# Inverting the triangular blocks of an RWKV recurrence in two stages: side 16 on VectorE, side 32 on TensorE

## The chip, the cores and the metric

The kernel runs on one core of a Trainium2 chip. The metric is the device time of one execution in microseconds (us). A core has TensorE (PE in the profile, with its weight loads as PEld), VectorE (DVE), ScalarE (ACT), GpSimd (POOL) and SyncE (SP), which here only issues transfers.

## What is computed

The program is a two-layer backbone (model width 1024, 256 latent and 256 context tokens, 4-byte floats). Layer 0 has retention beside grouped-query attention and a dense feed-forward part; layer 1 has differential attention beside a bidirectional RWKV-7 recurrence, and then top-2-of-8 experts. The change touches the recurrence. For each of 8 heads of width 64 and in each of two directions, the reference runs over the tokens:

```python
def step(s, inp):
    rt, wt, kt, vt, at, bt = inp
    s_new = (s * wt[:, :, None, :]
             + jnp.einsum('bhvk,bhk->bhv', s, at)[..., None] * bt[:, :, None, :]
             + vt[..., None] * kt[:, :, None, :])
    y = jnp.einsum('bhvk,bhk->bhv', s if read_before else s_new, rt)
    return s_new, y
```

The kernel computes this in chunks of 64 tokens. Inside a chunk, the term with `a` and `b` makes each token depend on the earlier ones of the chunk, which is a unit triangular system of side 64 for each chunk, head and direction. The kernel inverts these matrices ahead of the scan.

## The kernel before

Tokens come in two halves of 256, half 0 the context and half 1 the latent tokens. A half has 4 chunks, 8 heads and 2 directions: 64 triangular matrices of side 64, each with two diagonal blocks of side 32 and one block off the diagonal. The stages of `layer1` from about 840 to 1090 us of the profile, in their order:

- `prep(d, half)` makes the decayed operands AR (`a` and `r`) and BK (`b` and `k`) of a direction, with ScalarE's exponentials and sigmoids and, on VectorE, scalings of 256 elements (L966) and operations of 1024 (L950, L962 to L972).
- `inv_blocks(half)` (L992) makes the diagonal blocks (`dg`, L1008) and those off the diagonal (`off`, L1011) by small products on quadrants of the array, copies them to Lc and Lo on ScalarE, and with a transpose of 32x32 blocks on VectorE (L1018) brings Lc into M: one diagonal block of side 32 to a partition, 128 in all.
- `inv_diag(half, cut)` (L1022) inverts all 128 blocks at once by forward substitution, N = (I - M)^-1, in 31 steps. A step is a product (tile tmv or tmg, L1037) and an addition into N (L1039). The columns of N below `cut` are VectorE's, the others GpSimd's; `cut` is 2 for half 0 and 8 for half 1.
- `inv_join(half)` (L1044) turns N back with two transposes on VectorE (X0 and X1, L1048 and L1049), copies the blocks into XF (L1055), and finds the block off the diagonal with two sets of 64 small products, `gp` (L1063) and `wp` (L1072). ScalarE copies gp to Gs and wp into XF (L1077).
- `chain(half)` runs the recurrence, four times a step for both directions. `step` (L1111) has products lm, transposes tp, then z (from the state), u (XF times z), s (the new state), and for half 1 the output Y.

`weave` writes several generators side by side: the inversion of half 0 beside prep and inv_blocks of half 1, the inversion and joining of half 1 beside chain(0). chain(1) follows, then the output projection with `moe_open`, which starts the stream of expert weights (L1411) that runs to the end. The order in which an engine gets its instructions is set by a scheduler of the framework from this program; each engine then works in that order. PSUM banks are named by use (`banks`): before, `acc` takes three banks in turn during the inversion of half 0 and then six.

Of the kernel before, what the change touches and what calls it, by code (L numbers as in the profile page):

```python
# [19 lines left out]
FFN = 2816  # L20
# [8 lines left out]
# columns of a diagonal block's inversion that the vector engine takes from GpSimd, per half  # L29
CUT0, CUT1 = 2, 8  # L30
# how the modulation is spread: over the FFN (yields, start), with gqa, with the retention
# [3 lines left out]
# buffers that hold weights until their own use comes, and the last chunk that may lie there  # L35
# [3 lines left out]
def _constants():  # L39
# [18 lines left out]
    parts["hind"] = hind.reshape(128, 32)  # L58
    def rope(dim):
        rows = SEQ // GRID_W  # L60
        row = np.repeat(np.arange(rows, dtype=f), GRID_W)
        col = np.tile(np.arange(GRID_W, dtype=f), rows)
        n = dim // 4
        fr = f(10000.0) ** (-np.arange(n, dtype=f) / f(n))
        ang = np.concatenate([row[:, None] * fr, col[:, None] * fr], axis=-1).astype(f)
        return np.cos(ang).astype(f), np.sin(ang).astype(f)
# [29 lines left out]
def weave(*parts):  # L96
    """emits generators side by side; each part is (generator, its number of yields, where it starts)"""
    live = [[float(at[0]) if at else 0.0, i, g, n] for i, (g, n, *at) in enumerate(parts)]
    while live:
        p = min(live)  # L100
        try:
            next(p[2])
            p[0] += 1.0 / p[3]
        except StopIteration:
            live.remove(p)
# [25 lines left out]
def _build(top, tc, nc, V, S, G, T, I, O):  # L131
# [22 lines left out]
    def banks(**by_use):  # L154
        """which PSUM banks each use takes in turn"""
        use.update(by_use)
# [7 lines left out]
    acc, tpp, att, ybank = (bank(k) for k in ("acc", "tp", "at", "y"))  # L164
    banks(acc=range(6), tp=(6, 7))
# [32 lines left out]
    def columns(name, parts):  # L198
        """the given rows of 128 as columns"""
        n = sum(p[2] for p in parts)  # L200
        rows = xnp0.tile([n, 128], F32, name=name + "_r")
        r0 = 0
        for nm, src, k in parts:
            nc.scalar.dma_start(rows[r0:r0 + k], src)
            voff[nm] = r0
            r0 += k
        out = const_([128, n], name)
        t0 = tpp()
        T.transpose(t0[:, 0:n], rows, ident[0:n, 0:n])
        V.tensor_copy(out, t0[:, 0:n])  # L210
        return out
# [65 lines left out]
    def mod(layer):  # L277
# [4 lines left out]
        def put(q, tv):  # L282
            """section q in columns, as the norms' scales and shifts"""
            if q == 1:
                o = voff["ng"] + layer * 32
                ng = vec[:, o:o + 8].rearrange("p (s b) -> p b s", s=2)
                for r in range(2):
                    V.scalar_tensor_tensor(by_half(A1)[:, :, :, r], tv[:, :, :, r], 1.0, ng, op0=ALU.add, op1=ALU.mult)
            else:
                V.tensor_copy(by_half({0: B1, 3: B2, 4: A2}[q]), tv[:, :, :, 0:2])  # L290
# [12 lines left out]
        def first_two(pool):  # L303
            """sections 0 and 1 on the tensor engine: row r of slice s of 512 on partition 32 s + r"""
# [18 lines left out]
        def section(q):  # L323
            """1024 modulation columns, the products on the vector engine and their sums over the partitions on the
            tensor engine: row r of half s on partition 32 s + r, from section 2 on with the norm's factor:
            gate * g | shift | (1 + scale) * g | gate * g"""
# [41 lines left out]
        def rowb(pool, n, r, name, tag=None, q=nc.scalar):  # L368
            """section n's row for stream r on all partitions"""
            t = pool.tile([128, D], F32, name=name, tag=tag or name, bufs=1)  # L370
            bcast_rows(t, I["mrow"][layer, n // 2 - 1, r, n % 2 * 1024:n % 2 * 1024 + 1024], q)
            return t
# [3 lines left out]
    def norm_stats(xnp, blks):  # L376
        """rstd [128, blocks] and the normalized blocks"""
# [31 lines left out]
    def proj_tok(wsrc, n0, blks, fin, off=0, chunks=range(4), src=None, bmajor=False, out=None, spare=None):  # L409
        """token-major h @ w[:, n0:n0+512]; fin(b, PSUM tile) takes each block"""  # L410
# [24 lines left out]
    def post_norm_add(xnp, y, b, gb):  # L435
        """X[:, b] += rmsnorm(y) * gb with y two PSUM banks or SBUF halves"""
# [44 lines left out]
    def softmax(pool, sc, n, scale):  # L481
        """normalized exp over the free axis of a PSUM score tile"""
# [233 lines left out]
    def ffn0(first):  # L716
# [26 lines left out]
        def down(half, blks):  # L743
            """the blocks, both column halves, added to what the other half left"""
# [15 lines left out]
        def down_all(half):  # L760
            """all blocks, a column half at a time"""
# [29 lines left out]
    def layer1():  # L791
# [33 lines left out]
        def shift(i, a, dst, segs):  # L825
            """token shift of feature tile i from PSUM a[:, segs * 256] to dst [128, segs, 256]"""
# [8 lines left out]
        def project(i0):  # L835
            """feature-major tiles i0, i0 + 1 of the shifted projection"""
# [49 lines left out]
        def lora_weights(d):  # L886
            """rows of the other direction are zero, and so is what it adds"""
# [10 lines left out]
        def unit_keys():  # L898
            """minus the keys: k * k_k over its norm per head, which is found once per head and spread by a product"""
# [23 lines left out]
        def prep(d, half):  # L923
            """decayed operands of a direction: AR = (a | r), BK = (b | k), feature-major by chunk"""
# [63 lines left out]
        bn = lambda name: qI.tile([128, 32, 32], F32, name=name, tag="bn", bufs=5)  # L988
# [3 lines left out]
        def inv_blocks(half):  # L992
            """the 32 x 32 diagonal blocks of all chunks of a half, one to a partition, and those off the diagonal"""
            Lc = bn("Lc")
            off = acc("off")
# [21 lines left out]
            M = bn("M")  # L1017
            V.transpose(M.rearrange("p r c -> p c r"), Lc.rearrange("p u c -> p c u"))  # L1018
            iv[half] = M, Lo
            yield  # L1020

        def inv_diag(half, cut):  # L1022
            """forward substitution, columns shared by two engines: N becomes the inverse of I - M in each partition"""
            M, Lo = iv[half]
            N = bn("N")
            G.memset(flat(N), 0.0)
            G.memset(flat(N)[:, 0:1024:33], 1.0)
            for t in range(31):
                for eng, name, j0, j1 in ((V, "tmv", 0, cut), (G, "tmg", cut, 31)):
                    j1 = min(j1, t + 1)  # L1030
                    if j1 <= j0:
                        continue
                    tm = qI.tile([128, 256], F32, name=name, tag=name, bufs=2)
                    n, m = 31 - t, j1 - j0
                    tv = tm[:, 0:n * m].rearrange("p (i j) -> p i j", i=n)
                    Nv = N[:, t + 1:32, j0:j1]
                    eng.tensor_tensor(tv, M[:, t + 1:32, t:t + 1].to_broadcast([128, n, m]),  # L1037
                                      N[:, t:t + 1, j0:j1].to_broadcast([128, n, m]), op=ALU.mult)
                    eng.tensor_tensor(Nv, Nv, tv, op=ALU.add)  # L1039
                yield  # L1040
            iv[half] = N, Lo
            yield

        def inv_join(half):  # L1044
            """XF: transposed inverses of the unit triangular systems of all chunks of a half"""
            N, Lo = iv[half]
            X0, X1 = bn("X0"), bn("X1")
            V.transpose(X0.rearrange("p u c -> p c u"), N.rearrange("p r c -> p c r"))  # L1048
            V.transpose(X1.rearrange("p u r -> p r u"), N)  # L1049
            yield  # L1050
# [7 lines left out]
            Gs = qI.tile([128, 16, 32], F32, name="Gs", tag="Gs", bufs=1)  # L1058
# [22 lines left out]
        banks(acc=(3, 4, 5), at=(0, 1, 2))  # L1081
        drain(inv_blocks(0))
        weave((seq(prep(0, 1), prep(1, 1), inv_blocks(1)), 19), (inv_diag(0, CUT0), 32))
# [4 lines left out]
        for b in range(2):  # L1088
# [3 lines left out]
            V.tensor_copy(bon[:, b], t[:, 0:8])  # L1092
        banks(acc=range(6))
        drain(inv_join(0))
# [117 lines left out]
        weave((chain(0), 16), (seq(inv_diag(1, CUT1), inv_join(1)), 32))  # L1212
# [20 lines left out]
        def finish():  # L1233
            """what the last steps need besides the scan: (y * ln_g + ln_b + bonus) * gate = y * G1 + G2"""
# [68 lines left out]
    def diff(W, oD):  # L1303
        """projects for the differential attention; its pool and a generator of the attention"""
# [76 lines left out]
    def moe_open(rowb):  # L1381
        """what the experts need early: the stream of their weights and the modulation rows"""
# [30 lines left out]
        def ahead(c):  # L1413
            """loads what has its place free once chunk c - 1 is used"""
# [19 lines left out]
    def route_weights():  # L1434
        """logits = rstd * (x @ rt) + rb"""
# [8 lines left out]
    def moe():  # L1444
# [21 lines left out]
        def pre_split(eng=V):  # L1466
            """the next chunk into hi and lo parts, one [128, n] pair per row block"""
# [13 lines left out]
        def marks(g, q):  # L1481
            """one-hot: which row goes to which place of experts 2 g and 2 g + 1"""
# [22 lines left out]
        def warm(n):  # L1505
            """keeps the array's clock up where it would wait"""
# [11 lines left out]
        def turned(b):  # L1518
            """a block feature-major, and its sums of squares"""
# [92 lines left out]
        def gate_weights():  # L1612
            """softmax of the two logits, and the counts"""
# [19 lines left out]
        def gather(g, k2s=range(4)):  # L1633
            """the rows of experts 2 g and 2 g + 1, side by side, feature-major"""
# [136 lines left out]
    def sqrt_table():  # L1771
        """has the table of the last norm loaded ahead of it"""
# [3 lines left out]
    def overflow(mc, h2, gts, slotv, cnt, cmx, yacc, wg, wu, wd):  # L1776
        """rows of an expert beyond its first 128"""
# [96 lines left out]
```

## Time and profile before

| | us |
|---|---|
| three runs | 2152.70, 2155.31, 2157.81 |
| median | 2155.31 |
| profiled execution, first to last instruction | 2153.4 |
| TensorE busy | 2045.5 (95%) |
| VectorE busy | 1663.8 (77%) |
| ScalarE busy | 1220.2 (57%) |
| GpSimd busy | 166.0 (8%) |

The profile is one execution; its span is 1.9 us below the median of the runs. "Busy" is the time in which an instruction of that engine ran. A share over the whole span mixes stages with different limits, so stretches and timelines are read below. In a timeline, a row can stand for several equal instructions (x64); a bracket gives the idle time of the engine ahead of it and what ended that. "issue" means that nothing that the profile shows ended it. The granted clock (PEclk) is TensorE's, 1.00 for 2.4 GHz and 0.50 for 1.2 GHz.

### The profile page before, as it was taken

To read this page: it belongs to the slowest core of one execution; us is meant where nothing else is said; L and a number is where in the kernel's file an instruction comes from. 1 tells how busy PE (TensorE), PEld (TensorE's weight loads), DVE (VectorE), ACT (ScalarE), POOL (GpSimd) and SP (SyncE) were. 2 spreads that over 40 slices of the span, in tenths; PEclk is the share of its full clock that TensorE was granted. 3 is DMA by queue.
4 is the path that set the end of the run, shared out by engine and by line. 5 is a ranking of instruction groups with operands and counts; after the bars stand their busy time and mean duration, and the time that the engine had idled before them with its cause. 6 is when DMAs were issued, how large, how long until landed. Compare 5 with 4: busy or idle time off the path is not lost. (4 is left out here: it accounts for less than half of the span.)

```text
span 2153.4 us, 30029 instructions
## 1 busy us (share of the span) xinstructions
PE 2045.5 (95%) x11521; PEld 1635.4 (76%) x11522; DVE 1663.8 (77%) x2099; ACT 1220.2 (57%) x1581; POOL 166.0 (8%) x223
## 2 busy tenths in 40 slices
PE   6999989999999999858999999999999999999997
PEld 2767778777887766748887888888888787888875
DVE  3977783674557556688568999889989999899987
ACT  3543342222235445633337777777777777777775
POOL 0211110000000110284001000000000000000000
PEclk8999999999999999969999999999999999999999
DMA  8435351475645331101077999999999999999993
GB/s 297 160 109 168 110 172 55 152 244 187 203 150 166 111 88 45 36 16 51 21 268 258 366 317 350 332 347 367 355 343 352 350 372 347 339 352 357 366 353 144
DMA packets 224202, 493.99 MB, mean 229 GB/s; under 512 B 11355, under 2 KB 45262, under 8 KB 224054
## 3 DMA queue, kind: packets, MB, share of 16 engines
q1 hardware_dynamic: 219968, 482.62, 64.4%
q10 hardware_dynamic: 4086, 9.40, 1.3%
q8 instruction: 92, 1.51, 0.3%
q14 instruction: 56, 0.46, 0.1%
HBM read 490.87 MB, written 1.11 MB: 228 GB/s over the span
## 5 line engine op out<-in xcount | busy, mean ns | idle before, releaser
L273 DVE TENSOR_TENSOR mlo<-mraw,mhi 128x1024 fp32r<-128x1024 f32 x668 | 789.1, 1221 | 79.2 <-ACT mhi L272 62.4
L272 ACT ACTIVATE mhi<-mraw 128x1024 fp32r<-128x1024 f32 x668 | 682.9, 1057 | 104.3 <-PE y L269 49.0
L262 ACT ACTIVATE whi<-raw 128x1024 fp32r<-128x1024 f32 (+1 forms) x150 | 153.0, 1024 | 279.6 <-PE acc L269 109.6
L263 DVE TENSOR_TENSOR wlo<-raw,whi 128x1024 fp32r<-128x1024 f32 (+1 forms) x146 | 175.1, 1203 | 137.8 <-ACT whi L262 137.4
L267 PE MATMUL acc<-hTh,whi 128*128 128x512 f32 (+1 forms) x504 | 190.7, 380 | 0.0
L268 PE MATMUL acc<-hTl,whi 128*128 128x512 f32 (+1 forms) x504 | 186.6, 371 | 0.0
L269 PE MATMUL acc<-hTh,wlo 128*128 128x512 f32 (+1 forms) x504 | 185.6, 369 | 0.0
L268 PE MATMUL g<-mlo,xh 128*128 128x512 f32 x448 | 182.5, 407 | 0.3 <-POOL mlo L1581 0.3
L337 DVE SCALAR_TENSOR_TENSOR part<-mraw,cond,part 128x1024 f32<-128x1024 f32 x112 | 147.8, 1341 | 40.3 <-DMA mraw<-in_mod_w 40.2
L267 PE MATMUL g<-mhi,xh 128*128 128x512 f32 x448 | 178.6, 399 | 0.0
L267 PE MATMUL u<-mhi,xh 128*128 128x512 f32 x448 | 177.3, 396 | 0.0
L268 PE MATMUL u<-mlo,xh 128*128 128x512 f32 x448 | 177.3, 396 | 0.0
L269 PE MATMUL u<-mhi,xl 128*128 128x512 f32 x448 | 177.1, 395 | 0.0
L269 PE MATMUL g<-mhi,xl 128*128 128x512 f32 x448 | 177.1, 395 | 0.0
L268 PE MATMUL y<-mlo,acts 128*128 128x512 f32 x448 | 175.7, 392 | 0.3 <-DVE mlo L273 0.3
L269 PE MATMUL y<-mhi,acts 128*128 128x512 f32 x448 | 174.8, 390 | 0.0
L267 PE MATMUL y<-mhi,acts 128*128 128x512 f32 x448 | 151.4, 390 | 0.0
L267 PE MATMUL acc<-whi,hTh 128*128 128x512 f32 x336 | 137.7, 413 | 5.3 <-ACT whi L262 3.4
L268 PE MATMUL acc<-wlo,hTh 128*128 128x512 f32 x336 | 135.8, 404 | 4.5 <-DVE wlo L263 4.5
L269 PE MATMUL acc<-whi,hTl 128*128 128x512 f32 x336 | 134.7, 402 | 0.0
L267 PEld LDWEIGHTS acc<-hTh,whi 128*128 128x128 f32 x504 | 95.3, 190 | 22.4 <-issue 4.1
L268 PEld LDWEIGHTS acc<-hTl,whi 128*128 128x128 f32 x504 | 95.0, 189 | 17.6 <-issue 2.8
(437 smaller groups left out, 3510.1 us busy)
## 6 DMA issues: line engine op xcount, KB each, us to landing
mraw<-in_moe_w_gate SPq DMA_DIRECT2D x112, 1024.0 KB
mraw<-in_moe_w_up SPq DMA_DIRECT2D x112, 1024.0 KB
mraw<-in_moe_w_down SPq DMA_DIRECT2D x110, 1024.0 KB
mraw<-in_mod_w SPq DMA_DIRECT2D x96, 512.0 KB
raw<-in_ffn_w_down SPq DMA_DIRECT2D x32, 512.0 KB
raw<-in_odd_w_in SPq DMA_DIRECT2D x26, 512.0 KB
raw<-in_even_w_in SPq DMA_DIRECT2D x24, 512.0 KB
raw<-in_ffn_w_gate SPq DMA_DIRECT2D x20, 512.0 KB
```

The lines of the kernel that those rows point to most:

```text
L262: S.activation(h, v, AF.Copy)
L263: (eng or V).tensor_tensor(l, v, h, op=ALU.subtract)
L267: T.matmul(out, ah, bh, start=first, stop=False)
L268: T.matmul(out, ah, bl, start=False, stop=False)
L269: T.matmul(out, al, bh, start=False, stop=last)
L272: S.activation(hi, src, AF.Copy)
L273: eng.tensor_tensor(lo, src, hi, op=ALU.subtract)
L337: V.scalar_tensor_tensor(part[r], w, c_, part[r], op0=ALU.mult, op1=ALU.add)
```

## The change

Each diagonal block of side 32 is taken as two blocks of side 16 on the diagonal and one off it. `inv_diag` inverts the two blocks of 16 in each partition with the same VectorE operations (a further axis x of 2), in 15 steps; GpSimd has no part in it. The block off the diagonal is then found by TensorE in `inv_join`: `dc` is Lc times the right half of X1, ScalarE copies it to DC (with a mask of 0 and 1 by row, a new constant low16), and two sets of products, both called x, give what is added into X0 and X1. Each set has 128 products with a stationary 32x32 and a moving 32x16, on the four diagonal quadrants of the array in turn. After that the joining to side 64 goes on as before. The big tiles now have named places (`places`) in place of a ring of five, `acc` has two banks and then five where it had three and six, and `off` has a bank of its own.

```diff
-        bn = lambda name: qI.tile([128, 32, 32], F32, name=name, tag="bn", bufs=5)
+        places = ({"M": 0, "N": 1, "X0": 3, "X1": 0, "DC": 1, "Gs": 1}, {"M": 2, "N": 3, "X0": 0, "X1": 1, "DC": 2, "Gs": 2})
+        bnt = lambda name, half: qI.tile([128, 2, 528], F32, name=name, tag=f"bn{places[half][name]}", bufs=1)
+        whole = lambda x: x.rearrange("p x f -> p (x f)")[:, 0:1024].rearrange("p (a b) -> p a b", a=32)
+        diag16 = lambda x: x[:, :, 0:512].rearrange("p x (r c) -> p x r c", c=32)[:, :, :, 0:16]
+        bn = lambda name, half: whole(bnt(name, half))
...
-            for t in range(31):
-                for eng, name, j0, j1 in ((V, "tmv", 0, cut), (G, "tmg", cut, 31)):
-                    j1 = min(j1, t + 1)
-                    if j1 <= j0:
-                        continue
-                    tm = qI.tile([128, 256], F32, name=name, tag=name, bufs=2)
-                    n, m = 31 - t, j1 - j0
-                    tv = tm[:, 0:n * m].rearrange("p (i j) -> p i j", i=n)
-                    Nv = N[:, t + 1:32, j0:j1]
-                    eng.tensor_tensor(tv, M[:, t + 1:32, t:t + 1].to_broadcast([128, n, m]),
-                                      N[:, t:t + 1, j0:j1].to_broadcast([128, n, m]), op=ALU.mult)
-                    eng.tensor_tensor(Nv, Nv, tv, op=ALU.add)
+            Md, Nd = diag16(M), diag16(N)
+            for t in range(15):
+                tm = qI.tile([128, 128], F32, name="tmv", tag="tmv", bufs=2)
+                n, m = 15 - t, t + 1
+                tv = tm[:, 0:2 * n * m].rearrange("p (x i j) -> p x i j", x=2, i=n)
+                Nv = Nd[:, :, t + 1:16, 0:m]
+                V.tensor_tensor(tv, Md[:, :, t + 1:16, t:t + 1].to_broadcast([128, 2, n, m]),
+                                Nd[:, :, t:t + 1, 0:m].to_broadcast([128, 2, n, m]), op=ALU.mult)
+                V.tensor_tensor(Nv, Nv, tv, op=ALU.add)
                 yield
...
             V.transpose(X1.rearrange("p u r -> p r u"), N)
             yield
+            quads = [(32 * x, u) for u in range(32) for x in range(4)]
+
+            def small(name, lhs, rhs):
+                a = acc(name)
+                for o_, u in quads:
+                    T.matmul(a[o_:o_ + 32, u * 16:u * 16 + 16], lhs[o_:o_ + 32, u], rhs[o_:o_ + 32, u],
+                             start=True, stop=True, tile_position=(o_, o_))
+                return a.rearrange("p (u r) -> p u r", u=32)
+            DC = bn("DC", half)
+            G.memset(DC[:, :, 0:16], 0.0)
+            a = small("dc", Lc, X1[:, :, 16:32])
+            S.activation(DC[:, :, 16:32], a, AF.Copy, scale=rc("low16"))
+            yield
+            a0 = small("x0", DC, X0[:, :, 0:16])
+            a1 = small("x1", X0, DC[:, :, 16:32])
+            V.tensor_tensor(X0[:, :, 0:16], X0[:, :, 0:16], a0, op=ALU.add)
+            V.tensor_tensor(X1[:, :, 16:32], X1[:, :, 16:32], a1, op=ALU.add)
+            yield
...
-        banks(acc=(3, 4, 5), at=(0, 1, 2))
+        banks(acc=(3, 4), at=(0, 1, 2), off=(5,))
         drain(inv_blocks(0))
-        weave((seq(prep(0, 1), prep(1, 1), inv_blocks(1)), 19), (inv_diag(0, CUT0), 32))
+        weave((seq(prep(0, 1), prep(1, 1), inv_blocks(1)), 19), (inv_diag(0), 16))
...
+        banks(acc=range(5))
+        drain(inv_join(0))
         banks(acc=range(6))
-        drain(inv_join(0))
...
-        weave((chain(0), 16), (seq(inv_diag(1, CUT1), inv_join(1)), 32))
+        weave((chain(0), 16), (seq(inv_diag(1), inv_join(1)), 21))
```

How the scheduler's order moves is seen at two places of TensorE's queue (an operation is named by the tile that it writes, then those that it reads; x counts products; the line numbers are those of the kernel before or of the changed one, which stand some 23 lines apart).

TensorE at the joining of half 0, before:

```order
L1139 MATMUL tp<-cst_all,vT 128x128 x4
L1126 MATMUL lm<-pad_7760,BK_6335 128x128 x4
L1132 MATMUL tp<-cst_all,BK_6338 128x128 x4
L1139 MATMUL tp<-cst_all,vT 128x128 x4
L1132 MATMUL tp<-cst_all,BK_6335 128x128 x4
L1149 MATMUL z<-UV,Lm 64x64 x8
L1139 MATMUL tp<-cst_all,vT 128x128 x2
L1063 MATMUL gp<-X_7608,Lo 32x32 x32
L1139 MATMUL tp<-cst_all,vT 128x128 x2
L1132 MATMUL tp<-cst_all,BK_6338 128x128 x2
```

The same place with the change:

```order
L1162 MATMUL tp<-cst_all,vT 128x128 x4
L1155 MATMUL tp<-cst_all,BK_6338 128x128
L1060 MATMUL dc<-X_7474,Lc 32x16 x128
L1155 MATMUL tp<-cst_all,BK_6338 128x128 x3
L1162 MATMUL tp<-cst_all,vT 128x128 x4
L1060 MATMUL x_7609<-X_7473,DC 32x16 x128
L1060 MATMUL x_7738<-DC,X_7473 32x16 x128
L1155 MATMUL tp<-cst_all,BK_6335 128x128 x4
L1162 MATMUL tp<-cst_all,vT 128x128 x4
L1085 MATMUL gp<-X_7473,Lo 32x32 x32
L1085 MATMUL gp<-X_7474,Lo 32x32 x32
```

The products lm and z of the recurrence stood between and ahead of gp. Now dc and both x come ahead of gp, the transposes tp between them, and lm and z behind.

TensorE at the end of the recurrence over half 0, before:

```order
L1152 MATMUL z<-St,pad_7763 64x64
L1162 MATMUL u<-zpad_7764,XF_6860 64x64 x8
L1139 MATMUL tp<-cst_all,vT 128x128 x2
L1063 MATMUL gp<-X_8447,Lo 32x32 x12
L1172 MATMUL s<-UV,bkt 64x64
L1162 MATMUL u<-zpad_7765,XF_6860 64x64
L1172 MATMUL s<-UV,bkt 64x64
L1063 MATMUL gp<-X_8447,Lo 32x32 x3
L1162 MATMUL u<-zpad_7765,XF_6860 64x64 x7
L1063 MATMUL gp<-X_8447,Lo 32x32 x16
L1172 MATMUL s<-UV,bkt 64x64 x8
```

The same place with the change (17 more of dc stand ahead of the z):

```order
L1172 MATMUL z<-UV,Lm 64x64
L1175 MATMUL z<-St,pad_8020 64x64
L1060 MATMUL dc<-X_8542,Lc 32x16 x111
L1185 MATMUL u<-zpad_8021,XF_6860 64x64 x8
L1185 MATMUL u<-zpad_8022,XF_6860 64x64 x8
L1060 MATMUL x_8699<-X_8541,DC 32x16 x128
L1060 MATMUL x_8828<-DC,X_8541 32x16 x128
L1195 MATMUL s<-UV,bkt 64x64 x16
L1085 MATMUL gp<-X_8541,Lo 32x32 x32
L1085 MATMUL gp<-X_8542,Lo 32x32 x32
```

gp was mixed with the last u and s. Now dc stands ahead of u, both x between u and s, and all of gp behind s.

## Rows read from the trace of the kernel before

**Rows 1.** The page: busy time of the engines; an instruction queue (packets, MB, share).

```profile
PE 2045.5 (95%) x11521; PEld 1635.4 (76%) x11522; DVE 1663.8 (77%) x2099; ACT 1220.2 (57%) x1581; POOL 166.0 (8%) x223
...
q8 instruction: 92, 1.51, 0.3%
```

**Rows 2.** Busy us (x instructions) of PE, PEld, DVE, ACT, POOL; PEclk, DMA share, GB/s.

```profile
930.00:950.00 20.00, 8.44 (x215) 8.30 (x216) 19.34 (x40) 0.60 (x1) 18.26 (x23) 0.50 0.07 15
...
970.00:1010.00 40.00, 36.37 (x565) 34.25 (x561) 33.69 (x98) 13.48 (x30) 14.37 (x35) 0.96 0.05 16
```

**Rows 3.** Timeline of VectorE (start us, us, line, operation), with one row on tile tmv.

```profile
905.05 2.07 DVE L1018 STREAM_TRANSPOSE M<-Lc 128x1024 f32<-128x1024 f32 x1 [4.46 <-ACT Lc L1013]
...
913.83 1.21 DVE L962 TENSOR_TENSOR BK<-tb,En 128x1024 f32<-128x1024 f32 x1
914.96 0.50 DVE L1037 TENSOR_TENSOR tmv<-M,N 128x50 f32<-128x50 f32 x1
...
945.48 0.47 DVE L1086 SCALAR_TENSOR_TENSOR rkT<-rT,vec,kT 128x256 f32<-128x256 f32 x1
...
961.55 0.15 DVE L1039 TENSOR_TENSOR N<-N,tmv 128x2 f32<-128x2 f32 x1
...
963.67 1.99 DVE L1049 STREAM_TRANSPOSE X<-N 128x1024 f32<-128x1024 f32 x1
...
L1037 DVE TENSOR_TENSOR tmv<-M,N x62: 144/298/632, 907.2 to 1007.1; 128x31 f32<-128x31 f32 x2, 128x60 f32<-128x60 f32 x2, 128x56 f32<-128x56 f32 x2, 128x48 f32<-128x48 f32 x2
```

**Rows 4.** Timelines of TensorE and ScalarE, joining of half 0, first z.

```profile
964.29 1.20 PE L1063 MATMUL gp<-X,Lo 32*32 32x32 f32 x64
...
966.00 1.20 PE L1063 MATMUL gp<-X,Lo 32*32 32x32 f32 x64
...
975.80 0.76 PE L1149 MATMUL z<-UV,Lm 128*64 128x64 f32 x13 [3.05 <-DVE Lm L1128]
...
971.00 2.40 ACT L1077 ACTIVATE XF<-wp 32x512 f32<-32x512 f32 x4 [0.40 <-PE wp L1072]
```

**Rows 5.** TensorE, dg and off: timeline, and two stretches (columns as in rows 2).

```profile
895.26 0.76 PE L1008 MATMUL dg<-BK,AR 64*32 64x32 f32 x64
...
897.98 0.25 PE L1008 MATMUL dg<-BK,AR 64*32 64x32 f32 x5 [0.75 <-issue]
...
901.98 0.28 PE L1008 MATMUL dg<-AR,BK 64*32 64x32 f32 x5 [2.45 <-issue]
...
897.90:901.90 4.00, 1.55 (x128) 1.44 (x128) 2.68 (x4) 1.60 (x4) 0.00 (x0) 0.98 0.24 64
...
937.00:940.70 3.70, 3.61 (x192) 3.53 (x192) 3.70 (x7) 0.00 (x0) 3.54 (x3) 0.50 0.02 4
```

**Rows 6.** DMA in 894 to 908 us: rate in 40 slots, and the instruction queue.

```profile
GB/s 0 0 0 0 0 47 0 0 0 0 0 0 0 0 0 0 47 0 70 211 181 140 123 23 0 0 0 47 0 0 0 0 0 0 0 0 0 0 47 0
...
q8 instruction: 4, 0.07, 1.6%
```

**Rows 7.** Timelines of TensorE and ScalarE, joining of half 1, first product of chain(1).

```profile
1017.38 1.89 PE L1072 MATMUL wp<-X,Gs 32*32 32x32 f32 x77 [0.47 <-issue]
1022.51 0.77 PE L1126 MATMUL lm<-pad,BK 128*128 128x256 f32 x1 [3.24 <-DVE pad L1118]
...
1019.31 2.38 ACT L1077 ACTIVATE XF<-wp 32x512 f32<-32x512 f32 x4 [2.38 <-PE wp L1072]
```

**Rows 8.** What starts the expert weights: SyncE's waits and issues, and three stretches.

```profile
SPq L240 <- PE Y L1189: 19.3, 1, 19.3
...
1090.99 1.38 SPq L1411 DMA_DIRECT2D mraw<-in_moe_w_gate  x1
...
1040.00:1060.00 20.00, 20.00 (x278) 18.20 (x277) 11.02 (x22) 6.52 (x14) 1.48 (x2) 1.00 0.01 2
1100.00:1110.00 10.00, 9.24 (x51) 7.51 (x50) 7.11 (x9) 3.20 (x4) 0.00 (x0) 1.00 1.02 374
2000.00:2100.00 100.00, 100.00 (x443) 80.33 (x442) 89.49 (x87) 75.78 (x83) 0.00 (x0) 1.00 0.99 357
```

More of the change, by code (lines that the diff above doesn't have):

```diff
@@ L28 @@
 RAW = 8
-CUT0, CUT1 = 2, 8
 NM, N0 = 72, 0.1
@@ L58, in _constants @@
     parts["hind"] = hind.reshape(128, 32)
+    parts["low16"] = (i[:, None] % 32 < 16).astype(f)
     def rope(dim):
@@ L164, in _build @@
     acc, tpp, att, ybank = (bank(k) for k in ("acc", "tp", "at", "y"))
+    offb = bank("off")
     banks(acc=range(6), tp=(6, 7))
@@ L992, in inv_blocks @@
         def inv_blocks(half):
-            Lc = bn("Lc")
-            off = acc("off")
+            Lc = qI.tile([128, 32, 32], F32, name="Lc", tag="Lc", bufs=2)
+            off = offb("off")
             for d in range(2):
@@ L1016, in inv_blocks @@
             S.activation(flat(Lo), off, AF.Copy)
-            M = bn("M")
-            V.transpose(M.rearrange("p r c -> p c r"), Lc.rearrange("p u c -> p c u"))
-            iv[half] = M, Lo
+            M = bnt("M", half)
+            V.transpose(whole(M).rearrange("p r c -> p c r"), Lc.rearrange("p u c -> p c u"))
+            iv[half] = M, Lc, Lo
             yield
[L1022 to L1027, printed above, removed]
-            for t in range(31):
-                for eng, name, j0, j1 in ((V, "tmv", 0, cut), (G, "tmg", cut, 31)):
-                    j1 = min(j1, t + 1)
-                    if j1 <= j0:
-                        continue
-                    tm = qI.tile([128, 256], F32, name=name, tag=name, bufs=2)
-                    n, m = 31 - t, j1 - j0
-                    tv = tm[:, 0:n * m].rearrange("p (i j) -> p i j", i=n)
-                    Nv = N[:, t + 1:32, j0:j1]
-                    eng.tensor_tensor(tv, M[:, t + 1:32, t:t + 1].to_broadcast([128, n, m]),
-                                      N[:, t:t + 1, j0:j1].to_broadcast([128, n, m]), op=ALU.mult)
-                    eng.tensor_tensor(Nv, Nv, tv, op=ALU.add)
@@ new lines, in inv_diag @@
+        def inv_diag(half):
+            M, Lc, Lo = iv[half]
+            N = bnt("N", half)
+            G.memset(whole(N), 0.0)
+            G.memset(flat(whole(N))[:, 0:1024:33], 1.0)
+            Md, Nd = diag16(M), diag16(N)
[7 more added lines that the diff above has]
+                V.tensor_tensor(Nv, Nv, tv, op=ALU.add)
@@ L1040, in inv_diag @@
                 yield
-            iv[half] = N, Lo
+            iv[half] = whole(N), Lc, Lo
             yield
         def inv_join(half):
-            N, Lo = iv[half]
-            X0, X1 = bn("X0"), bn("X1")
+            N, Lc, Lo = iv[half]
+            X0, X1 = bn("X0", half), bn("X1", half)
             V.transpose(X0.rearrange("p u c -> p c u"), N.rearrange("p r c -> p c r"))
             V.transpose(X1.rearrange("p u r -> p r u"), N)
+            yield
+            quads = [(32 * x, u) for u in range(32) for x in range(4)]
@@ L1057, in inv_join @@
             gp = acc("gp")
-            Gs = qI.tile([128, 16, 32], F32, name="Gs", tag="Gs", bufs=1)
+            Gs = bn("Gs", half)[:, 0:16]
             for d in range(2):
```

## Prediction

> **What bounds the kernel now.** I read the totals first, then busy time by stretch, then the timelines of the inversion, then the transfers behind it. TensorE is busy 95% of the span [rows 1], but that is a mean over stages. In 930 to 950 us it works 8.4 of 20 us at a granted clock of 0.50, VectorE 19.3 and GpSimd 18.3 of 20 [rows 2]. There the 31 steps of the inversion of half 0 run, on those two engines. Its matrix M is ready at 907.1, the last column of N at 961.7; the second of the two transposes that follow ends at 965.7 [rows 3]. Then come the joining products gp and wp, and ScalarE's copies end XF of half 0 at 973.4 [rows 4]. The recurrence over half 0 (chain(0)) follows, with TensorE busy 36.4 of the 40 us from 970 to 1010 at clock 0.96 [rows 2]: there one product more costs time, and a VectorE operation less hardly saves any. It ends with the joining of half 1, whose XF is ready at 1021.7, and the first product of chain(1) starts at 1022.5 [rows 7].
>
> What this stage gains or loses reaches the end. The rows loaded just ahead of the expert weights wait for the last product of chain(1) (19.3 us on Y), the first expert weights are issued at 1091.0, and the DMA engines are idle before (0.01) and full behind (1.02, and still 0.99 at 2000 to 2100) [rows 8]. So I pass every microsecond on in full.
>
> **What is removed.** Step 1, the inversion of half 0. GpSimd's part goes; 30 VectorE operations remain, with 30 to 128 elements. The old ones on VectorE take 0.30 us in the median of 62 [rows 3]: 30 x 0.30 = 9.0. In its new order VectorE has beside them, up to the second transpose: twelve operations of 1024 elements at 1.21 (14.5), twelve of 256 at 0.47 (5.6), M of half 1 (2.0), the two transposes (4.1) [rows 3], and two of 512 with a few small copies (1.8, an estimate between those rows). Together 37.0. Neighbours overlap by 0.08 (the operation at 914.96 starts 1.13 after one that takes 1.21 [rows 3]), some 28 times: 2.2 off, 34.8 left. VectorE also waits for the last diagonal block of half 1, but the 0.30 still holds GpSimd's company; I let the two cancel. So the second transpose ends at 907.1 + 34.8 = 941.9, **23.8 us earlier**.
>
> Step 2, the inversion of half 1 shrinks too. It lies beside chain(0), which TensorE bounds. I count nothing; the cover is TensorE's own 36 us. N of half 1 now has the place of X0 of half 0, so its memset waits for the last wp of half 0, the first step of the inversion for that, and a copy of the recurrence is queued behind it on VectorE. But chain(0) was held up there before too (its z waited 3.0 us for VectorE's Lm [rows 4]); nothing for this either.
>
> **What is added.** Step 3: for each half three sets of 128 products of 32x32 by 32x16, dc and the two called x. The trace shows that a product of 4-byte floats is two matmuls: gp is 64 products in the code and 64 + 64 in the timeline [rows 4]. So there are 768 matmuls a half, **1536 in all**, each with its own weight load. The trace has none of this shape; p, the time of one, decides the case.
>
> The nearest row is dg: four quadrants of the array in turn, as dc and x use them. Undisturbed it takes 9.0 ns at full clock (64 in 0.76 us, less 0.19 for the last alone) and, with its companion off, 18.8 ns at clock 0.50 (192 in 3.61 us) [rows 5]. But it doesn't keep that pace. At 897.98 a stop of 0.75 us ends, at 901.98 one of 2.45, both put down to "issue", a wait that the profile can't name; between the two ends lie 4.0 us with exactly 128 matmuls and 128 loads [rows 5]. In the same stretch the instruction queue moves four packets, evenly 3.9 us apart (the four 47s in a line whose 40 slots are 0.35 us each) [rows 6]. Over the program it moves 92 packets for TensorE's 11,521 + 11,522 instructions, 250 each [rows 1]. So a packet holds some 256 instructions, and a second one comes no sooner than about 4.0 us after the first: 31.2 ns a matmul. wp of half 1 stops in the same way (0.47) [rows 7]. Long matmuls never show this; 1536 tiny ones are twelve packets, 48 us of delivery.
>
> The Trainium skill (Runtime: NRT & Kernel Launch, "Instruction fetch mechanics") describes blocks of 16 KiB with 256 instructions, and says that the fetch is hidden because instructions are dispatched more slowly than the buffer fills. By that rule p would be dg's undisturbed pace and the change a gain, the first rival below. The two stops speak against it, and the measurement decides.
>
> I take p = 31.2 ns, from the stretch with stops, since dc and x are longer unbroken runs (256 and 512 matmuls) than dg's.
>
> Step 4, what stands in line with them. Half 0: DC's copy out of PSUM (0.6, as its like in rows 4, where XF's four take 2.40) and the second addition into X (0.7), with their handing over 1.7; and the first half of gp, which ran beside the second transpose (1.20 [rows 4]), now follows the additions, with a little waiting 1.4. Half 1: DC's copy lies beside u and the additions beside s; gp no longer fills waits ahead of s, 1.0 (an estimate below the 1.20). Sum 4.1. DC's memset is hidden by GpSimd's idleness.
>
> **The sum.** 1536 p - 23.8 + 4.1 = 47.9 - 19.7 = +28.2. Off this comes what hides the delivery: half 0 starts with a packet in hand (128 x (31.2 - 18.8) = 1.6) and fetches during the 1.7 of step 4; half 1 fetches ahead during z and u, whose matmuls have 64 columns and are slower than the delivery (2.4, an estimate of less than a packet). That is 5.7, which leaves **+22.5 us**: XF of half 0 some 3 us later than now, the rest lost between there and chain(1). The profiled execution's span is 2153.4, 1.9 below the median of 2155.3; the median goes to **2177.8**.
>
> Ends: p = 18.8, with nothing taken off, gives +9.2 (2164). p = 31.2 with nothing hidden, and a clock of 0.50 while TensorE starves, as in 930 to 950 [rows 2], doubles u, s, gp and wp at the end of half 0's chain (some 8 us): +36 (2191).
>
> **Rivals.**
> 1. Instructions come in time and the quadrants run at 9.0 ns: 1536 x 0.009 - 19.7 = -5.9, **2149**. For it: 192 matmuls at 937 run without a stop [rows 5], so over one packet can be in hand. Against it: dc with x is six packets in a row. It is what the page's rule gives. It decides at p below 12.8 ns, a packet every 1.64 us. Chance 0.12.
> 2. The price lands near that break-even (p from 10 to 15.6 ns): within 0.2%, **2155**. 0.2% (4.3 us) is about what a measurement of this kernel can tell from no change. Chance 0.07.
> 3. The quadrants don't overlap. gp alternates between two and takes (1.20 - 0.19) / 63 = 16 ns, so one alone 32, and twice that at half clock. At 37.5 the sum is +37.9, **2193**. Against it: dg at 9.0. Chance 0.09.
>
> **How the numbers follow.** The forecast has 0.72 and 2164 to 2191 as its own range. A range from 2153 to 2194 holds it, the upper part of rival 2 and about half of rival 3; it leaves out rival 1 and a tail, 0.18 or so. Faster 0.12 (rival 1), same 0.07 (rival 2), slower 0.81.
>
> **What would show it.** The second transpose of half 0 ends near 942 (step 1). dc and x come in groups of 128 matmuls that start 3.9 to 4.0 us apart with "issue" between, and the page has 104 instruction packets for TensorE, not 92 (step 3). XF of half 0 near 976, the first product of chain(1) near 1045, the first expert weights near 1113. I am wrong if the 256 matmuls of dc take under 4 us without "issue", if XF of half 0 is ready before 970, or if chain(0)'s last s ends before 1024.

## Result and profile after

| | us |
|---|---|
| before, median of 4 runs | 2154.5 |
| with the change, median of 4 runs | 2176.8 (2173.3 to 2178.3) |
| ratio, with its 95% interval | 1.0097 (1.0082 to 1.0112) |
| profiled execution, before and after | 2153.4 and 2176.4 |
| predicted | 2177.8 |

The change costs 22 us. The page of the changed kernel, its engines and its instruction queue for TensorE, against [rows 1]:

```profile
PE 2070.7 (95%) x13057; PEld 1658.0 (76%) x13058; DVE 1633.7 (75%) x2039; ACT 1221.4 (56%) x1583; POOL 108.4 (5%) x121
...
q8 instruction: 104, 1.70, 0.3%
```

TensorE has 1536 matmuls and 12 instruction packets more; its share of busy time, 95%, says nothing of either. The timeline of VectorE, which answers to [rows 3]:

```profile
936.91 2.09 DVE L1051 STREAM_TRANSPOSE X<-N 128x1024 f32<-128x1024 f32 x1
939.59 1.95 DVE L1052 STREAM_TRANSPOSE X<-N 128x1024 f32<-128x1024 f32 x1
962.86 0.69 DVE L1070 TENSOR_TENSOR X<-X,x 128x512 f32<-128x512 f32 x1 [18.95 <-PE x L1060]
```

The short inversion is done at 941.5 where the old one needed 965.7. Then VectorE waits 18.95 us for TensorE's small products. What TensorE does in that time, and for half 1, shows its timeline (start, us, line, tile, count; a bracket is the idle time ahead):

```profile
941.60 2.22 PE L1060 MATMUL dc<-X,Lc 32*32 32x16 f32 x150
945.72 1.67 PE L1060 MATMUL dc<-X,Lc 32*32 32x16 f32 x106 [1.91 <-issue]
...
949.63 1.91 PE L1060 MATMUL x<-X,DC 32*32 32x16 f32 x128 [0.22 <-issue]
953.64 1.73 PE L1060 MATMUL x<-X,DC 32*32 32x16 f32 x114 [2.10 <-issue]
...
957.37 1.90 PE L1060 MATMUL x<-DC,X 32*32 32x16 f32 x128 [1.82 <-issue]
961.09 1.73 PE L1060 MATMUL x<-DC,X 32*32 32x16 f32 x114 [1.83 <-issue]
...
964.65 3.44 PE L1085 MATMUL gp<-X,Lo 32*32 32x32 f32 x128
...
1008.86 1.99 PE L1060 MATMUL dc<-X,Lc 32*32 32x16 f32 x217
1013.36 0.30 PE L1060 MATMUL dc<-X,Lc 32*32 32x16 f32 x5 [2.50 <-issue]
1013.59 3.67 PE L1185 MATMUL u<-zpad,XF 128*64 128x64 f32 x32
1017.20 3.16 PE L1060 MATMUL x<-X,DC 32*32 32x16 f32 x219
1025.19 0.67 PE L1060 MATMUL x<-X,DC 32*32 32x16 f32 x35 [4.83 <-issue]
...
1028.92 1.90 PE L1060 MATMUL x<-DC,X 32*32 32x16 f32 x128 [1.83 <-issue]
1032.66 0.72 PE L1060 MATMUL x<-DC,X 32*32 32x16 f32 x37 [1.84 <-issue]
...
1045.93 4.35 PE L1149 MATMUL lm<-pad,BK 128*128 128x256 f32 x10 [3.85 <-DVE pad L1141]
```

Read the starts: 945.72, 949.63, 953.64, 957.37, 961.09 lie 3.7 to 4.0 us apart, with 128 matmuls from one to the next, of which the array needs 1.9. That is the pace of dg in [rows 5]. The transfers of 945 to 965 us, in 40 slots of 0.5 us, are the instruction packets alone:

```profile
GB/s 0 0 0 33 0 0 0 0 0 0 0 33 0 0 0 0 0 0 0 33 0 0 0 0 0 0 33 0 0 0 0 0 0 0 33 0 0 0 0 0
...
q8 instruction: 5, 0.08, 1.9%
```

Each packet moves about 1 us after a group of 128 has begun, and 2.6 to 2.9 us before the next group begins. So the groups and the packets go in step. What the sets cost in all is in two views: the busy time of x, then of dc, by stretch (half 0 and half 1; columns as in [rows 2], of the engines that take part), and TensorE's waits from 930 to 1050 us (total, times, longest):

```profile
935.00:963.00 28.00, 7.84 (x512) 7.30 (x512) 0.14 (x1) 0.50 0.10 32
1005.35:1033.30 27.95, 7.60 (x512) 7.26 (x512) 0.00 (x0) 0.63 0.24 79
...
935.00:963.00 28.00, 3.89 (x256) 3.67 (x256) 0.69 (x1) 0.50 0.10 32
1005.35:1033.30 27.95, 2.77 (x256) 2.47 (x256) 0.69 (x1) 0.63 0.24 79
```

```profile
PE x L1060 <- issue: 14.5, 7, 4.8
PE dc L1060 <- issue: 4.4, 2, 2.5
```

The 1536 matmuls keep the array busy 22.1 us (7.84 + 7.60 + 3.89 + 2.77) and stop it for 18.9: 41.0 us, 26.7 ns each. What follows them: ScalarE's copies into XF, half 0 and half 1, and SyncE's first expert weights:

```profile
973.24 2.39 ACT L1099 ACTIVATE XF<-wp 32x512 f32<-32x512 f32 x4 [4.02 <-PE wp L1094]
1041.76 2.39 ACT L1099 ACTIVATE XF<-wp 32x512 f32<-32x512 f32 x4 [2.01 <-PE wp L1094]
```

```profile
1113.66 1.21 SPq L1434 DMA_DIRECT2D mraw<-in_moe_w_gate  x1
```

XF of half 0 is 2.2 us later than in [rows 4], XF of half 1 22.5 later than in [rows 7], the expert weights 22.7 later than in [rows 8]. Nothing is made up after that.

### The profile page after: what moved, and what is told of

It reads as the page before. It is cut to its first block, busy times and chain, and to the rows that moved or that the text cites. A ratio compares the mean times of both kernels' runs of the same rounds, so it can differ in the third digit from the quotient of the medians.

```text
span 2176.4 us, 32941 instructions
## 1 busy us (share of the span) xinstructions
PE 2070.7 (95%) x13057; PEld 1658.0 (76%) x13058; DVE 1633.7 (75%) x2039; ACT 1221.4 (56%) x1583; POOL 108.4 (5%) x121
## 5 line engine op out<-in xcount | busy, mean ns | idle before, releaser
L262 ACT ACTIVATE whi<-raw 128x1024 fp32r<-128x1024 f32 (+1 forms) x150 | 152.9, 1024 | 280.1 <-PE acc L269 104.8
L267 PEld LDWEIGHTS acc<-hTh,whi 128*128 128x128 f32 x504 | 95.1, 190 | 22.7 <-issue 4.1
```

The lines of the kernel that those rows point to most:

```text
L262: S.activation(h, v, AF.Copy)
L267: T.matmul(out, ah, bh, start=first, stop=False)
```

## Experiments

The theory to test: what costs is the delivery of instructions, 256 in some 3.8 us, so a matmul with its load in a long run of tiny ones costs 30 ns whatever it computes. Rivals: the array's own time for the sets; the clock; a fixed cost of the sets (their waits and hand-overs). All runs are timed beside the kernel before.

| run | what it is | median, us | ratio to before (95%) |
|---|---|---|---|
| wide32 | 32 moving columns for 16 | 2178.6 | 1.0104 (1.0087 to 1.0121) |
| few128 | an eighth of the products, 128 columns | 2141.1 | 0.9931 (0.9914 to 0.9947) |
| half0_new | half 1 as before | 2158.1 | 1.0017 (1.0008 to 1.0027) |
| half1_new | half 0 as before | 2175.9 | 1.0091 (1.0065 to 1.0116) |
| tr | x1 by a transpose | 2162.8 | 1.0032 (1.0018 to 1.0046) |
| half0_new_tr | the same, half 1 as before | 2157.6 | 1.0014 (1.0004 to 1.0024) |
| mixed | sets of half 1 spread out | 2164.7 | 1.0041 (1.0027 to 1.0055) |
| mixed_tr | spread out, x1 by a transpose | 2152.0 | 0.9982 (0.9968 to 0.9995) |
| late_load | weight loads held back | 2174.7 | 1.0079 (1.0064 to 1.0095) |
| half1_early | best version | 2143.8 | 0.9939 (0.9926 to 0.9953) |
| before_early | its control | 2161.5 | 1.0024 (1.0014 to 1.0034) |

### Instructions or columns

wide32 doubles the columns and keeps the instructions (in both x as in dc):

```diff
-                    T.matmul(a[o_:o_ + 32, u * 16:u * 16 + 16], ...
+                    T.matmul(a[o_:o_ + 32, u % 16 * 32:u % 16 * 32 + 32], ...
...
-            a = small("dc", Lc, X1[:, :, 16:32])
+            a = small("dc", Lc, X1)
...
```

> The changed kernel with 32 moving columns in each product of dc and x where it has 16: the same 1536 matmuls and loads, twice the columns. The results of u and u + 16 are written over each other, so this part of the numbers is not the reference's. Theory of the supply (a packet of 256 instructions comes no sooner than some 3.8 us after the one before, whatever the instructions do): as the changed kernel, 2177 us, within 3. Rival, the array's own time (p grows with the columns): the 768 matmuls of a half at twice the price of the columns, up to 20 us more, about 2190. In the profile the theory asks for dc in pieces of 128 with 'issue' between, starting 3.7 to 4.0 us apart as before.

few128 keeps the columns and has an eighth of the instructions:

```diff
-            quads = [(32 * x, u) for u in range(32) for x in range(4)]
+            quads = [(32 * x, u) for u in range(0, 32, 8) for x in range(4)]
...
-                    T.matmul(a[o_:o_ + 32, u * 16:u * 16 + 16], lhs[o_:o_ + 32, u], rhs[o_:o_ + 32, u],
+                    T.matmul(a[o_:o_ + 32, u * 16:u * 16 + 128], lhs[o_:o_ + 32, u], rhs[o_:o_ + 32, u:u + 8],
```

> The changed kernel with one product of 128 columns in place of eight of 16: 16 products a set, 1344 matmuls and 1344 loads fewer in all, the same number of columns through the array. It uses the stationary of every eighth block only, so the joining to side 32 is left out in part and the numbers are not the reference's. Theory of the supply: the stops go, a set takes well under 2 us, the instruction queue has 11 packets fewer (93 or 94), and the time falls to some 2140, range 2135 to 2147. Rival, the array's own time for these columns or the clock: unchanged at 2177, or not under 2165.

Measured: 2178.6 and 2141.1, both as the theory has it. wide32 against the changed kernel, 2176.8, is no difference that this measurement can tell. Its sets by line, 935 to 1050 us (busy, mean ns of one, idle ahead):

```profile
L1060 PE MATMUL x<-DC,X 32*32 32x32 f32 x512 | 7.7, 229 | 9.0 <-issue 9.0
L1060 PE MATMUL dc<-X,Lc 32*32 32x32 f32 x512 | 6.7, 215 | 4.0 <-issue 4.0
L1060 PE MATMUL x<-X,DC 32*32 32x32 f32 x512 | 6.7, 216 | 5.2 <-issue 5.2
```

The stops are 18.2 us, about as long as with 16 columns (18.9). The array time is no longer either, 21.1 us against 22.1: from 16 to 32 columns it goes with the number of matmuls. So this run rules out the columns; whether the stops go with the number of instructions is for few128 to show. The timeline of few128, both halves, and its instruction queue:

```profile
940.26 1.49 PE L1060 MATMUL dc<-X,Lc 32*32 32x128 f32 x32
...
942.67 1.08 PE L1060 MATMUL x<-X,DC 32*32 32x128 f32 x32
943.54 1.08 PE L1060 MATMUL x<-DC,X 32*32 32x128 f32 x32
...
945.57 2.12 PE L1085 MATMUL gp<-X,Lo 32*32 32x32 f32 x128
...
999.93 0.37 PE L1085 MATMUL gp<-X,Lo 32*32 32x32 f32 x5 [4.63 <-issue]
```

```profile
q8 instruction: 94, 1.54, 0.3%
```

The three sets of half 0 take 4.4 us where they took 21.2, without a stop. And gp takes 2.12 us where the changed kernel's took 3.44 for the same 128 matmuls. The granted clock was low ahead of the sets in both (0.52 in the changed kernel from 930 to 941.6, 0.50 in few128 from 935 to 940). In few128 it rose, to 0.89 in 940.2 to 944.7 and 1.00 behind. In the changed kernel TensorE comes out of its stops at half clock and stays at it: in the stretch from 962.8 to 970.8 it is busy without a gap, at a granted clock of 0.50:

```profile
941.60:962.80 21.20, 13.32 (x776) 12.37 (x776) 2.31 (x4) 3.18 (x7) 4.64 (x8) 0.50 0.07 17
962.80:970.80 8.00, 8.00 (x149) 7.46 (x148) 4.46 (x10) 2.27 (x4) 0.00 (x0) 0.50 0.02 4
```

In half 1 the clock fell at the stops: 0.92 in 1005.35 to 1013.6, 0.50 in the 3.6 us of u behind the first of them. So the stops have a second price, paid by the work behind them. Of few128's 35.6 us, 14.8 are array time (7.3 against 22.1) and 14.3 are stops (4.6 against 18.9); of the rest, 6.5, the half clock of gp, lm, u and s is 5.3 by their durations, given below.

### Which half

half0_new and half1_new bring back the old inversion (`inv_diag` before, with its cut) for one half and leave out dc and x there:

```diff
-        weave((chain(0), 16), (seq(inv_diag(1), inv_join(1)), 21))
+        weave((chain(0), 16), (seq(inv_diag_old(1, 8), inv_join(1)), 32))
```

> Half 0 by the change, half 1 by the old inversion on VectorE and GpSimd, with the old cut of 8. By the prediction half 0 alone is ready some 3 us later than before and the rest of the loss belongs to half 1: 2157, range 2154 to 2161, so 17 to 20 below the changed kernel. Rival, the loss is in half 0 (its clock falls and drags chain(0) with it): 2167 or more.

> The complement: half 0 by the old inversion (cut 2), half 1 by the change. If the two halves add up (half 0 alone measured 3.1 over the kernel before, both together 22.3), this gives 2154.5 + 19.2 = 2173.7, range 2170 to 2177. Rival, half 1 is only slow because half 0 comes late or at a low clock: 2165 or less.

Measured 2158.1 and 2175.9. Half 0 alone costs some 3 us, half 1 alone some 20, and 3 + 20 is about what both cost (22.3). In half 0 the faster inversion nearly pays for the products; in half 1 nothing pays, since the inversion there lies beside TensorE's work (step 2 of the prediction).

### Fewer products, other places

tr drops one of the three sets of each half, half0_new_tr the same in half 0 with half 1 as before:

```diff
-            a1 = small("x1", X0, DC[:, :, 16:32])
...
-            V.tensor_tensor(X1[:, :, 16:32], X1[:, :, 16:32], a1, op=ALU.add)
+            V.transpose(X1, X0)
```

> The changed kernel with the second set of products, x1, replaced in both halves by a transpose on VectorE (X1 from X0 after its addition): 512 matmuls and 512 loads fewer, four packets. Half 0 gains 4 to 7.5 us (in the run with half 0 new, XF came 7.5 us earlier by it), half 1 another 4 to 7 less 1.4 on VectorE: 2165, range 2161 to 2169. Rival, the clock or the waits between the sets and not the number of instructions: under 4 us of gain, 2173 or more.

> As the run with half 0 new and half 1 old, and in half 0 the second set of products, x1, is replaced by one more transpose on VectorE (X1 from X0 after its addition). This takes 256 matmuls (4.0 us of supply by the prediction) out of half 0 and adds some 1.4 us on VectorE (2.0 for the transpose less 0.7 for the addition that goes). Theory of the supply: 2 to 3 us below that run, so 2153 to 2156, no more than the kernel before or just under. Rival, the loss of half 0 is not the products: no change against that run, or slower by the 1.4.

tr measured 2162.8, 14 us under the changed kernel for 512 matmuls less, 27 ns each. half0_new_tr is a miss: 2157.6 where 2153 to 2156 was expected, no gain over half0_new. In the profiled executions its XF of half 0 is ready 7.5 us sooner, that of half 1 only 3.2 sooner; the medians, 0.4 apart, show nothing of it. Its waits on TensorE (960 to 1030 us) point to where the head start went, to a place where GpSimd also runs the old inversion of half 1; half0_new has neither of these two waits:

```profile
PE z L1194 <- POOL UV L1181: 3.1, 2, 1.8
...
PE z L1194 <- POOL N L1064: 1.0, 1, 1.0
```

mixed keeps all 1536 matmuls and changes their places; mixed_tr does it with x1 by a transpose:

```diff
-        places = (..., {"M": 2, "N": 3, "X0": 0, "X1": 1, "DC": 2, "Gs": 2})
+        places = (..., {"M": 2, "N": 4, "X0": 0, "X1": 1, "DC": 2, "Gs": 2})
...
-                for o_, u in quads:
+                for i_, (o_, u) in enumerate(quads):
+                    if half and i_ % 32 == 0:
+                        yield
...
-        drain(inv_join(0))
+        weave((inv_join(0), 5), (inv_diag(1), 16))
...
-        weave((chain(0), 16), (seq(inv_diag(1), inv_join(1)), 21))
+        weave((chain(0), 16), (inv_join(1), 18))
```

In mixed_tr the last number is 14.

> The changed kernel with the same 1536 matmuls, in another order: N of half 1 has a place of its own, so its inversion runs on VectorE while TensorE joins half 0, and each set of dc and x of half 1 is cut into four pieces spread over the recurrence of half 0, among its longer matmuls. Theory of the supply: what counts is instructions per stretch, and those of the recurrence leave room. From the last wp of half 0 to that of half 1 some 1620 matmuls with their loads are 12.7 packets, at 3.8 us 48 us, so XF of half 1 is ready at about 1024 to 1030 and not at 1044: 2159, range 2155 to 2166. Rival, the time of the sets in the array or a fixed cost of each small product: the order does not matter, 2177, or not under 2172.

> Both together: the order of the run mixed, and x1 by a transpose. Half 0 ready some 7 us before the kernel before; then 1370 matmuls with their loads to the joining of half 1, 10.7 packets or 41 us, and TensorE's own work of some 40 us, so XF of half 1 at 1008 to 1014 and not at 1021.7 as in the kernel before: 2145, range 2140 to 2151, under both kernels. Rival, supply is not what counts: no better than the run tr, 2161 or more.

Measured 2164.7 and 2152.0: 12 us for the order alone, and 25 for both. The order matters, so it is no fixed cost of the products. Both gained less than expected: mixed by 6 us, within its range, mixed_tr by 7, which is 1 us outside it; it is under both kernels all the same. XF of half 1 was ready at 1039.0 and 1022.6, some 9 us later than expected (1024 to 1030 and 1008 to 1014). In mixed_tr TensorE is busy 49.4 of the 52.6 us from 970 to it, so its own work and not the delivery, which the expectation put at 41 us, set that time. The two sets of half 1 there (by line, 970 to 1050 us) stop for 2.4 us in all:

```profile
L1062 PE MATMUL dc<-X,Lc 32*32 32x16 f32 x256 | 3.2, 182 | 1.0 <-issue 1.0
L1062 PE MATMUL x<-X,DC 32*32 32x16 f32 x256 | 2.9, 180 | 1.4 <-issue 1.4
```

That is 8.5 us for 512 matmuls, 17 ns each: delivery is nearly hidden among matmuls of 64 and 128 columns, but the array time stays.

### The longest stop

One stop, 4.83 us, is twice the others. While it lasts the weights of the output projection come in. late_load holds them back:

```diff
+            if half:
+                V.tensor_copy(flag, X1[:, 0, 16:17])
...
+        if after is not None:
+            S.copy(raw[:, 0:1], after)
```

> The changed kernel with the eight loads of the output projection's weights held back until the additions into X1 of half 1 are done, some 1034 us, where they ran from 1018 to 1026. The order of TensorE is the same. Theory: the one long stop inside x of half 1 (4.83 us, 6.8 from piece to piece) is an instruction packet that comes late behind these 4 MB; without them it is like the others, 1.8 us and 3.7 to 3.8 from piece to piece, x ends 3 us earlier and the time is 2174, range 2171 to 2176, if the held loads do not make the recurrence after it wait. Rival: that stop has another cause (TensorE's own waiting at u just ahead, a jump in the program): it stays over 4 us, 2177.

One of the eight loads still ran there. The transfers of 1012 to 1036 us, in the changed kernel and then in late_load, and the stop in late_load's timeline:

```profile
GB/s 0 0 0 0 0 27 0 0 0 0 27 55 297 324 318 239 314 358 403 393 386 280 85 24 48 0 0 0 0 0 27 0 0 0 0 0 27 0 0 0
...
q1 hardware_dynamic: 1088, 2.10, 26.3%
```

```profile
GB/s 27 0 0 0 0 0 27 0 0 0 0 0 10 68 294 379 150 0 0 0 0 0 27 0 0 0 0 0 27 0 0 0 0 0 0 27 0 0 0 58
...
q1 hardware_dynamic: 289, 0.56, 9.7%
```

```profile
1024.34 0.67 PE L1063 MATMUL x<-X,DC 32*32 32x16 f32 x35 [2.66 <-issue]
...
1034.69 3.44 PE L1090 MATMUL gp<-X,Lo 32*32 32x32 f32 x128
```

With 0.56 MB in place of 2.10 the stop is 2.66. In the changed kernel one instruction packet moved at 1015.1 and the next only between 1022 and 1024, while the loads ran, where packets are otherwise 3.5 to 4 us apart. Other runs in which the loads met tiny products had such a stop too (few128 4.63, in gp; half1_new 4.5; tr 5.1); wide32 had two shorter ones, of 3.7 and 3.6. So a packet of instructions comes late while data are loaded. The time, 2174.7, is in its range but can't be told from 2176.8. In the profiled execution gp ran at half clock (3.44, in the changed kernel 2.28), which takes back 1.2 us of the 2.2 that the shorter stop gave.

### A version that beats both

Half 0 by the change with x1 by a transpose; half 1 by the old method, but with a place of its own for N, so that its 31 steps begin while TensorE joins half 0:

```diff
-        drain(inv_join(0))
+        weave((inv_join(0), 5), (inv_diag_old(1, 8), 32))
...
-        weave((chain(0), 16), (seq(inv_diag(1), inv_join(1)), 21))
+        weave((chain(0), 16), (inv_join(1), 6))
```

> Half 0 by the change with x1 by a transpose; half 1 by the old inversion, but with a place of its own for N, so that its 31 steps start on VectorE and GpSimd while TensorE joins half 0 with its tiny products. TensorE then has only gp and wp of half 1 inside the recurrence of half 0. XF of half 0 at 966 to 970 as in the run half0_new_tr, then some 37 us of TensorE work: XF of half 1 at 1006 to 1012 and not at 1021.7 as in the kernel before: 2142, range 2138 to 2148. Rival: VectorE and GpSimd cannot run ahead there (they are as busy as in the kernel before, or something else holds chain(1)): 2150 or more.

The control is the kernel before with that order alone:

```diff
-        drain(inv_join(0))
+        weave((inv_join(0), 4), (inv_diag(1, CUT1), 32))
...
-        weave((chain(0), 16), (seq(inv_diag(1, CUT1), inv_join(1)), 32))
+        weave((chain(0), 16), (inv_join(1), 4))
```

> A control for the run half1_early: the kernel before with only the order of that run, the inversion of half 1 put beside the joining of half 0 and not beside the recurrence. In the kernel before VectorE and GpSimd are full until N of half 0 is done at 961.7, so half 1 can start hardly earlier than it does now. Theory: most of half1_early's 12 us needs the free VectorE and GpSimd that the short inversion of half 0 leaves from 941 us on, so this is 2151 to 2156. Rival: the order alone does it, 2142 to 2147.

Measured 2143.8, 0.61% under the kernel before, and 2161.5 for the control, over it. The order alone loses, and half 0's part alone (half0_new_tr) gains nothing; the gain needs both, the order and VectorE and GpSimd free from 941 us on. The control is 5.5 us above its range. TensorE's granted clock there was 0.66 in 1000 to 1017 us, 1.00 in the kernel before; whether that is the whole reason isn't shown. Busy time of half1_early in 940 to 960 us (TensorE, loads, VectorE, ScalarE, GpSimd), and its XF of half 1:

```profile
940.00:960.00 20.00, 14.84 (x597) 13.31 (x597) 18.41 (x37) 5.75 (x11) 18.80 (x36) 0.50 0.06 18
```

```profile
994.49 2.39 ACT L1121 ACTIVATE XF<-wp 32x512 f32<-32x512 f32 x4 [1.69 <-PE wp L1116]
```

All three engines work where in the changed kernel VectorE waited 18.95 us, and XF of half 1 is ready at 996.9, 25 us sooner than in [rows 7] and 9 us or more sooner than expected, ahead of its need. Most of that lead is not used: the first product of chain(1) comes 6.0 us earlier (1016.51), the first expert weights 8.9 (1082.06).

## Why the prediction was right

- **Step 1 held, in part by luck.** The second transpose ended at 941.54, predicted 941.9; it removes 24.1 us. But M was ready at 908.0, not 907.1, and the stretch from there took 33.5 us, not 34.8; the 30 short operations alone took 7.5 where 9.0 was put. The errors cancel.
- **Step 2 held.** X of half 1 was ready at 997.9, and dc of half 1 came in TensorE's order at 1005.35: the shorter inversion gave nothing, as half1_new shows too. "Nothing" was right for this change only; half1_early shows that the free time of VectorE and GpSimd is worth 12 us to a kernel that puts something there.
- **Step 3 held in its mechanism; that its number came so near is luck.** Predicted 47.9 less 5.7 hidden, 42.2; measured 41.0. The page counts 104 packets. The groups of 128 start 3.7 to 4.0 us apart, not 3.9 to 4.0; twelve at 3.8 are 45.6, 2.3 less than predicted. The four packets of [rows 6] had this pace already: they lie 11, 11 and 10 slots apart, 3.7 us in the mean and not evenly 3.9. More was hidden than the 5.7: dc of half 1 ran 217 matmuls in 1.99 us without a stop, 1.7 packets, where the prediction had one in hand. Against that, one packet came 3 us late behind the weight loads, which no step had.
- **Step 4 was too small.** Predicted 4.1; 22.7 - 41.0 + 24.1 leaves 5.8. The prediction had the half clock only in its upper end, but it came: gp, lm, u and s took 3.44, 2.93, 3.67 and 2.58 us where few128, at or near full clock, has 2.12, 1.60, 2.08 and 1.54, 5.3 in all. The clock alone makes up most of what is left; how much of it stood beside hand-overs that step 4 had counted can't be read from the rows, so 4.1 came near 5.8 in part by luck.
- **The sum.** Predicted +22.5, measured +22.3 in the medians and +23.0 in the spans. XF of half 0 at 975.6 (976), the first product of chain(1) at 1045.9 (1045), the expert weights at 1113.7 (1113): every microsecond of the stage reached the end.
- **Rival 1** (instructions in time) is out by the stops. Its 2149 was tested by no run: few128, 14 us under the kernel before, no longer stops in the sets, but has only an eighth of their matmuls, and the array needed 22.1 us for all of them where rival 1 had 13.8. The rule of the Trainium skill (Runtime: NRT & Kernel Launch, "Instruction fetch mechanics"), that the cost of the fetch is mostly hidden, agrees with the long matmuls of this kernel, which show no such stop; it does not agree with the 18.9 us of stops where 768 tiny ones a half come close together. **Rival 2** (10 to 15.6 ns) is out by the 26.7 ns that were measured. **Rival 3** (no overlap of the quadrants) is out by 217 matmuls in 1.99 us, 9.2 ns each.

## What to carry to other kernels

Before a product is cut into many small ones, count instructions and not only columns: here 128 matmuls with their loads took 3.7 to 4.0 us in a long run, whether 16 or 32 columns wide. Here a small stop in the old trace, in a place with the same kind of instructions, showed this limit and gave its price. Where the small products can't be fewer, spread them among long ones, and put waiting work onto the engine that the change set free: the first halved the loss; the second, with half 1 left to the old method, made a gain.

## What the runs showed of the hardware, unexpected

- An instruction packet came late while other data were loaded: a stop of 4.83 us with 2.10 MB in the stretch, 2.66 with 0.56 MB.
- In 945 to 965 us each instruction packet moved about 1 us after a group of 128 tiny matmuls had begun, and the next group began 2.6 to 2.9 us behind it.
- After stops of 1.8 to 2.1 us every 3.8, TensorE stayed at a granted clock of 0.50 for 8 us in which it was busy without a gap.
- 217 tiny matmuls with their loads, 1.7 packets, ran in 1.99 us without a stop where their run began behind longer matmuls; 128 of them took 3.7 to 4.0 us once it went on.
